# A gated-recurrence layer: the branch product in two halves with two gates behind each, and two PSUM tiles for the gates

## The chip, the cores and the metric

The kernel runs on one core of one Trainium2 chip. The metric is the device time of one execution in microseconds (us); of several executions the median counts. The engines are named as the profile names them: PE is TensorE (matrix products), DVE is VectorE, ACT is ScalarE, POOL is GpSimd, SP is SyncE, which here only issues DMA transfers.

## What is computed

Two layers of a hybrid backbone over 512 latent and 256 context tokens with 1024 channels. The first layer is a bidirectional RG-LRU, the second a retention layer, which the change doesn't touch. Of the reference this is the part that matters:

```python
def rglru_scan(xs, w_r, b_r, w_i, b_i, lam, h0, reverse):
    r = sigmoid(block_product(xs, w_r) + b_r)
    i = sigmoid(block_product(xs, w_i) + b_i)
    log_a = -LRU_C * r * softplus(-lam)
    a = exp(log_a)
    b = sqrt(-expm1(2.0 * log_a)) * (i * xs)
    ...  # h[t] = a[t] * h[t-1] + b[t]

def mixer_lru(h, hc, ...):
    u = h @ w_in                          # 1024 -> 4096: 2048 for x, 2048 for the branch
    xl = dwconv(u[..., :W], conv_w, conv_b, LRU_PAD)
    ...                                   # both directions, context first, then latent
    y = ((lat[0] + lat[1]) * silu(u[..., W:])) @ w_out
```

Each product is made of float32 operands split into a high and a low part, as three matmuls that add up in PSUM.

## The kernel before

Channels lie on the partitions and the 768 tokens (256 context, 512 latent) side by side in a row. The 2048 channels of the recurrence are 16 channel tiles of 128. PSUM is cut into four tiles of 1024 columns (`slots`, L51), which the compiled program names ps_67 to ps_70. The list `rot` with `psum()` (L54) hands them out in rotation.

`iteration(c)` (L447) runs once for each channel tile c = 0 to 15, and works on several tiles at once:

- **x product** of tile c+2: eight blocks of 128 input channels, two halves of 384 tokens, three matmuls each, so 48 matmuls (`mm_in`, L290). `x_post` (L267) is the convolution: one ACT pass (L271) and six DVE passes (L275) that all read the PSUM tile.
- **branch product** of tile c+1 (`w_in[c+1, 1]`), again 48 matmuls. `g_post` (L285) is its SiLU: a sigmoid on ACT (L287) and a product on DVE (L288), which both read the PSUM tile.
- **four gates** of tile c, six matmuls each from the convolved x and its low part (xh, xlo, made by `x_split`, L278). One sigmoid on ACT (L482) reads each.
- **output units** (`wout_unit`, L431): iterations 4, 6, 8, 10, 12, 13, 14 and 15 have one, 5 and 9 have two, 0 to 3, 7 and 11 none (the table `UNITS`, L105). A unit is 48 matmuls on two PSUM tiles, read by four DVE passes (`gate_add`, L242).
- **the recurrence of tile c** on ACT and DVE: exp, tanh and square (L499, L500, L502), square root (L515), products (L503, L504, L518), scans (L520 to L524), the sum with the branch (L530, L531), and the split of the result into yh (ACT, L532) and yl (DVE, L533). Three changes of ACT's function table (ACT_TABLE_LOAD) lie in each iteration.

The order of an iteration on PE is x product, branch product, four gates, units. Each of the first six pieces takes the next PSUM tile of the rotation. With four tiles and no unit, the third gate takes the tile of the x product and the fourth that of the branch product, made just before. From iteration 3 on four tiles rotate; in iterations 1 and 2 the fourth is taken by the modulation's matmuls.

Weights are loaded by SP into a pool of four raw tiles (`wraw`), split into whi (ACT, L91) and wlo (DVE, L96, or ACT L93 and a transfer that adds) in pools of four; `take()` (L154) splits three ahead. In iterations 3 to 14 `row_steps` (L404) also loads rows of the next layer's modulation weights through the same four raw tiles and reduces each in one DVE pass (L414), three an iteration: `mod_pull()` stands behind the x product, behind the branch product and behind the gates.

The sequence on each engine is set by a scheduler from the program's order; each engine runs its own list strictly in order. After iteration 15 the last products of the layer run on the four PSUM tiles in the order `T` (L543); they need yl of tile 15.

Of the kernel before, what the change touches and what calls it, by code (L numbers as in the profile page):

```python
# [15 lines left out]
KD = D // P  # L16
# [3 lines left out]
CT = 16  # L20
# [23 lines left out]
def backbone(ctx: ExitStack, tc: tile.TileContext, xT, vec, trig, lru_mod_sc, lru_mod_gt, lru_w_in, lru_w_g, lru_w_out,  # L44
# [6 lines left out]
    slots = [psp.tile([P, 1024], F32, name=f"ps{i}") for i in range(4)]  # L51
    rot = [0, 1, 2, 3]

    def psum():  # L54
        i = rot.pop(0)
        rot.append(i)
        return slots[i]
# [43 lines left out]
    PULL = {1: 2, 2: 2}  # L101
# [3 lines left out]
    UNITS = {4: [0], 5: [1, 2], 6: [3], 8: [4], 9: [5, 6], 10: [7], 12: [8], 13: [9], 14: [10], 15: [11]}  # L105
# [48 lines left out]
    def take(n=1, ahead=3):  # L154
        i = pos[0]
        pos[0] += n
        split_to(i + ahead)
        got = ready[i:i + n]
        ready[i:i + n] = [None] * n
        return got if n > 1 else got[0]  # L160
# [84 lines left out]
    with ExitStack() as l0:  # L245
# [18 lines left out]
        hs, us, ys = [], {}, {}  # L264
# [20 lines left out]
        def g_post(c, u):  # L285
            t = sil[c] = r3.tile([P, NT], F32, tag="sil", name="sil")
            nc.scalar.activation(out=t, in_=u[:, 128:896], func=AF.Sigmoid)  # L287
            nc.vector.tensor_tensor(out=t, in0=u[:, 128:896], in1=t, op=ALU.mult)  # L288

        def mm_in(w, ps, ks=range(KD)):  # L290
            for k in ks:
                wk = [t[:, k * P:(k + 1) * P] for t in w]
                for a, b in halves:
                    mm3(ps[:, 128 + a:128 + b], wk, cut(hs[k], a, b), k == 0, k == KD - 1)
# [132 lines left out]
        def pull(it, n):  # L427
            for _ in range(n):
                next(it, None)

        def wout_unit(i):  # L431
            g, dp = divmod(i, 4)
            hi, lo = take()
            yk = [ys[4 * g + k] for k in range(4)]
            pss = [psum(), psum()]
            for ks in ((0, 1, 2), (3,)):
                for d in range(2):
                    for k in ks:
                        w = [t[:, k * 256 + d * P:k * 256 + (d + 1) * P] for t in (hi, lo)]
                        for a, b in halves:  # L440
                            mm3(pss[d][:, 128 + a:128 + b], w, cut(yk[k], a, b), k == 0, k == 3)
            for d in range(2):
                dt = 2 * dp + d
                gate_add(acc_c, dt, pss[d][:, 128:384], gate0[0][:, dt, :])
                gate_add(acc_l, dt, pss[d][:, 384:896], gate0[1][:, dt, :])

        def iteration(c):  # L447
            def mod_pull():
                pull(mod_it, PULL.get(c, 0))
                pull(row_it, 1 if c in ROWS else 0)  # L450

            if c == 1:
                rot[:] = [i for i in rot if i != 3]
            if c + 2 < CT:
                us[c + 2] = psum()
                mm_in(take(), us[c + 2])
                if c == 0:
                    g_post(0, gps)
                    x_post(0)
                    x_split(0)  # L460
                    x_post(1)
                x_post(c + 2)
                mod_pull()
            if c + 1 < CT:
                ps = psum()
                mm_in(take(), ps)
                g_post(c + 1, ps)
                mod_pull()
            xh, xlo = xs.pop(c)
            wg = take()  # L470
            ri = []
            units = list(UNITS.get(c, []))
            for q in range(4):
                if q == 2 and c in EARLY:
                    wout_unit(units.pop(0))
                ps = psum()
                w = [t[:, q * P:(q + 1) * P] for t in wg]
                for a, b in halves:
                    mm3(ps[:, 128 + a:128 + b], w, (xh[:, a:b], xlo[:, a:b]), True, True)
                t = e(f"g{q}")  # L480
                boff = (V_BR if q % 2 == 0 else V_BI) + (q // 2) * CT + c
                nc.scalar.activation(out=t, in_=ps[:, 128:896], func=AF.Sigmoid, bias=vt[:, boff:boff + 1])  # L482
                ri.append(t)
            if c + 1 < CT:
                x_split(c + 1)
            mod_pull()
            if c == max(PULL):
                pull(mod_it, 100)
                rot.append(3)
            if c == max(ROWS):  # L490
                pull(row_it, 100)
            for i in units:
                wout_unit(i)
            x = xl.pop(c)
            aa, qq, ix, qs = [], [], {}, {}
            for d in range(2):
                r = ri[2 * d]
                a = e("a")
                nc.scalar.activation(out=a, in_=r, func=AF.Exp, scale=sneg[:, d * CT + c:d * CT + c + 1])  # L499
                nc.scalar.activation(out=r, in_=r, func=AF.Tanh, scale=spos[:, d * CT + c:d * CT + c + 1])  # L500
                q = e("q")
                nc.scalar.activation(out=q, in_=a, func=AF.Square)  # L502
                ix[d] = nc.vector.tensor_tensor(out=ri[2 * d + 1], in0=ri[2 * d + 1], in1=x, op=ALU.mult)  # L503
                qs[d] = nc.vector.scalar_tensor_tensor(out=q, in0=q, scalar=1.0, in1=r, op0=ALU.add, op1=ALU.mult)  # L504
                aa.append(a)
                qq.append(q)
            if c == CT - 1:
                with tc.issue_after(ix[1].ins):
                    split_to(pos[0] + 3, dve=True)
                yt = [(yp.tile([P, NT], F32R, tag="yh", name="yh"), yp.tile([P, NT], F32R, tag="yl", name="yl")) for _ in range(3)]  # L510
                with tc.issue_after(qs[0].ins):
                    split_y(pos[0] + 4, yt, 0, True)
            for d in range(2):
                i, q, a = ri[2 * d + 1], qq[d], aa[d]
                nc.scalar.activation(out=q, in_=q, func=AF.Sqrt)  # L515
                if d and c < CT - 1:
                    nc.scalar.activation(out=warm, in_=q[:, 0:1], func=AF.Sigmoid)
                nc.vector.tensor_tensor(out=i, in0=i, in1=q, op=ALU.mult)  # L518
                if d == 0:
                    nc.vector.tensor_tensor_scan(out=q, data0=a, data1=i, initial=0.0, op0=ALU.mult, op1=ALU.add)  # L520
                else:
                    nc.vector.tensor_tensor_scan(out=q[:, 0:NC][:, ::-1], data0=a[:, 0:NC][:, ::-1],
                                                 data1=i[:, 0:NC][:, ::-1], initial=0.0, op0=ALU.mult, op1=ALU.add)
                    nc.vector.tensor_tensor_scan(out=q[:, NC:NT][:, ::-1], data0=a[:, NC:NT][:, ::-1],  # L524
                                                 data1=i[:, NC:NT][:, ::-1], initial=q[:, 0:1], op0=ALU.mult, op1=ALU.add)
            s, sl = qq[0], sil.pop(c)
            yh = yp.tile([P, NT], F32R, tag="yh", name="yh")
            yl = yp.tile([P, NT], F32R, tag="yl", name="yl")
            for a, b in ([(NC, NT), (0, NC)] if c == CT - 1 else [(0, NT)]):
                nc.vector.tensor_tensor(out=s[:, a:b], in0=s[:, a:b], in1=qq[1][:, a:b], op=ALU.add)  # L530
                nc.vector.tensor_tensor(out=s[:, a:b], in0=s[:, a:b], in1=sl[:, a:b], op=ALU.mult)  # L531
                nc.scalar.activation(out=yh[:, a:b], in_=s[:, a:b], func=AF.Copy)  # L532
                nc.vector.tensor_tensor(out=yl[:, a:b], in0=s[:, a:b], in1=yh[:, a:b].bitcast(F32), op=ALU.subtract)  # L533
            ys[c] = (yh, yl)
            if c == CT - 1:
                split_y(pos[0] + 5, yt, 1, False)
# [3 lines left out]

        base = pos[0]
        l0x.close()
        T = [slots[i] for i in (2, 3, 1, 0)]  # L543

        def half(t, d):
            return T[t][:, 512 * d:512 * d + 512]

# [37 lines left out]
        def ctx_mm(dt):  # L585
            return last_mm(T[dt // 4][:, 256 * (dt % 4):256 * (dt % 4) + 256], dt, range(4), slice(0, NC))

# [17 lines left out]
        def ctx_add(q):  # L605
            for j in range(4):
                dt = 4 * q + j
                gate_add(acc_c, dt, T[q][:, 256 * j:256 * j + 256], gate0[0][:, dt, :])

# [329 lines left out]
def _pack(i):  # L939
    import numpy as np  # L940

    def cols(a, n):
        return np.asarray(a).reshape(n, P).T

# [25 lines left out]
def _layout(i):  # L970
# [11 lines left out]
    rwo = g['ret_w_out'].reshape(4, 4, P, 4, 256).transpose(0, 3, 2, 1, 4).reshape(4, 4, P, 1024)  # L982
    xT = np.concatenate([g['ctx'][0], g['x'][0]], axis=0).T
    mw = g['lru_mod_w']
# [24 lines left out]
```

## Time and profile before

| | us |
|---|---|
| median of three runs | 1080.85 |
| the three runs | 1078.47, 1080.85, 1082.74 |
| the profiled execution | 1081.35 |
| its span, first to last instruction | 1079.5 |
| PE busy | 1049.4 |
| DVE busy | 709.7 |
| ACT busy | 604.1 |

The profiled execution lies 0.50 us above the median, and 1.85 us of it lie outside the span. PE's busy time counts each matmul to its modelled end, so what it could still gain is read from the gaps before its instructions and from the length of like stretches. The stretches used below run from the first gate of iteration c to the first gate of iteration c+1: they hold the gates and units of c, the x product of tile c+3 and the branch product of tile c+2.

### The profile page before, as it was taken

The numbers are of one execution on the slowest core, as the hardware profiler recorded it, in microseconds if no ns is written. First come the engines' busy times: TensorE is split into PE (matmuls) and PEld (weight loads), VectorE is DVE, ScalarE is ACT, GpSimd is POOL, SyncE is SP. The second block draws the span as 40 slices with busy tenths as digits, with TensorE's granted clock in tenths as the row PEclk, the third lists the DMA queues.
The fourth block names the chain that finished last, engine by engine and source line by source line (L and its number), as shares of the span: only waits on it lengthen the run. The fifth ranks groups of instructions, "written<-read, shape, count | busy, mean of one in ns | idle before, by whom it ended". The sixth has DMA issues, their size and how long they took to land.

```text
span 1079.5 us, 14058 instructions
## 1 busy us (share of the span) xinstructions
PE 1049.4 (97%) x5644; PEld 934.1 (87%) x5644; DVE 709.7 (66%) x1031; ACT 604.1 (56%) x782; POOL 29.1 (3%) x37
## 2 busy tenths in 40 slices
PE   8999999999999999999999999999999999999997
PEld 7898898899999999998888788888888888887887
DVE  4777668876687787888889836444554535643366
ACT  5557888777788578888364534124432234322354
POOL 0000000000000000000000000000000000000000
PEclk9999999999999999999999999999999999999999
DMA  9623637665757666432113412212122021220202
GB/s 359 231 81 113 190 78 209 178 166 148 187 161 173 162 165 156 122 109 78 50 56 124 154 67 71 94 40 78 39 78 98 20 79 59 75 97 4 78 1 78
DMA packets 36243, 121.71 MB, mean 113 GB/s; under 512 B 3793, under 2 KB 6993, under 8 KB 35153
## 3 DMA queue, kind: packets, MB, share of 16 engines
q1 hardware_dynamic: 31568, 104.03, 27.8%
q0 software_dynamic: 4608, 16.78, 9.1%
q8 instruction: 44, 0.72, 0.3%
q14 instruction: 23, 0.18, 0.1%
HBM read 118.70 MB, written 2.10 MB: 112 GB/s over the span
## 4 chain that ended last, share of the span: by engine, by line
PE 68%; DVE 13%; ACT 12%; issue 4%; DMA 3%; SPq 0%; DVEq 0%; ACTq 0%
PE ps L76 23%; PE ps L77 22%; PE ps L78 21%; DVE xl L275 2%; ACT a L499 2%; ACT g L500 2%; DVE g L518 2%; ACT g L482 2%; ACT q L502 1%; ACT L499 1%; ACT L515 1%; DVE q L524 1%; DMA wraw<-in_ret_mod_w_dram 1%; ACT q L515 1%; DVE q L530 1%
## 5 line engine op out<-in xcount | busy, mean ns | idle before, releaser
L76 PE MATMUL ps<-hl,whi 128*128 128x384 f32 (+2 forms) x816 | 284.9, 350 | 3.0 <-ACT g L482 1.5
L78 PE MATMUL ps<-hh,wlo 128*128 128x384 f32 (+2 forms) x816 | 282.8, 347 | 0.1
L77 PE MATMUL ps<-hh,whi 128*128 128x384 f32 (+2 forms) x816 | 282.9, 347 | 0.0
L91 ACT ACTIVATE whi<-wraw 128x1024 fp32r<-128x1024 f32 (+1 forms) x125 | 125.1, 1002 | 189.9 <-PE ps L77 163.5
L76 PEld LDWEIGHTS ps<-hl,whi 128*128 128x128 f32 x816 | 153.4, 188 | 19.1 <-DVE hl L239 3.1
L78 PEld LDWEIGHTS ps<-hh,wlo 128*128 128x128 f32 x816 | 153.4, 188 | 10.3 <-DVE wlo L96 0.6
L77 PEld LDWEIGHTS ps<-hh,whi 128*128 128x128 f32 x816 | 153.5, 188 | 9.5
L76 PE MATMUL ps<-yl,whi 128*128 128x384 f32 (+2 forms) x416 | 143.8, 348 | 3.9 <-DVE yl L533 1.8
L96 DVE TENSOR_TENSOR wlo<-wraw,whi 128x1024 fp32r<-128x1024 f32 (+1 forms) x94 | 106.1, 1130 | 59.6 <-ACT whi L91 58.2
L77 PE MATMUL ps<-yh,whi 128*128 128x384 f32 (+2 forms) x416 | 143.3, 345 | 0.0
L78 PE MATMUL ps<-yh,wlo 128*128 128x384 f32 (+2 forms) x416 | 141.6, 343 | 0.0
L76 PEld LDWEIGHTS ps<-yl,whi 128*128 128x128 f32 x416 | 78.6, 189 | 12.7 <-ACT g L482 3.0
L78 PEld LDWEIGHTS ps<-yh,wlo 128*128 128x128 f32 x416 | 78.8, 190 | 5.7
L77 PEld LDWEIGHTS ps<-yh,whi 128*128 128x128 f32 x416 | 78.9, 190 | 5.2
L76 PE MATMUL ps<-wlo,hh 128*128 128x512 f32 x192 | 75.1, 394 | 1.4 <-DVE rb L705 0.9
L77 PE MATMUL ps<-whi,hh 128*128 128x512 f32 x192 | 74.9, 390 | 0.0
L78 PE MATMUL ps<-whi,hl 128*128 128x512 f32 x192 | 74.3, 389 | 0.0
L482 ACT ACTIVATE g<-ps,vt 128x768 f32<-128x768 f32 x64 | 55.3, 898 | 5.4 <-PE ps L78 3.6
L275 DVE SCALAR_TENSOR_TENSOR xl<-ps,vt,xl 128x255 f32<-128x255 f32 (+1 forms) x96 | 54.3, 602 | 2.2 <-ACT xl L271 2.2
L76 PE MATMUL ps<-xlo,whi 128*128 128x384 f32 x128 | 45.0, 354 | 10.2 <-DVE xl L275 5.8
L414 DVE SCALAR_TENSOR_TENSOR wraw<-wraw,cr 128x1024 f32<-128x1024 f32 x32 | 39.0, 1218 | 17.4 <-DMA wraw<-in_ret_mod_w_dram 12.5
L504 DVE SCALAR_TENSOR_TENSOR q<-q,g 128x768 f32<-128x768 f32 x32 | 30.5, 954 | 28.5 <-ACT q L502 28.5
(208 smaller groups left out, 1647.9 us busy)
## 6 DMA issues: line engine op xcount, KB each, us to landing
wraw<-in_ret_w_in_dram SPq DMA_DIRECT2D x48, 512.0 KB, 3.5
wraw<-in_lru_w_in_dram SPq DMA_DIRECT2D x32, 512.0 KB, 4.5
wraw<-in_ret_mod_w_dram SPq DMA_DIRECT2D x32, 512.0 KB, 4.2
wlo<-in_lru_w_in_dram POOLq DMA_DIRECT2D x22, 512.0 KB, 5.7
mraw<-in_lru_mod_sc_dram SPq DMA_DIRECT2D x8, 1024.0 KB, 8.9
wraw<-in_lru_w_out_dram SPq DMA_DIRECT2D x16, 512.0 KB, 3.6
wraw<-in_ret_w_out_dram SPq DMA_DIRECT2D x16, 512.0 KB, 4.0
wlo<-in_lru_w_out_dram POOLq DMA_DIRECT2D x10, 512.0 KB, 5.6
```

Of the source, the lines that this page charges most:

```text
L76: nc.tensor.matmul(ps, lhsT=lhs[0], rhs=rhs[1], start=first, stop=False)
L77: nc.tensor.matmul(ps, lhsT=lhs[0], rhs=rhs[0], start=False, stop=False)
L78: return nc.tensor.matmul(ps, lhsT=lhs[1], rhs=rhs[0], start=False, stop=last)
L91: nc.scalar.activation(out=hi, in_=raw, func=AF.Copy)
L96: last_split[0] = nc.vector.tensor_tensor(out=lo, in0=raw, in1=hi.bitcast(F32), op=ALU.subtract)
L275: nc.vector.scalar_tensor_tensor(out=t[:, o0:o1], in0=u[:, o0 + sh:o1 + sh], scalar=cw[j], in1=t[:, o0:o1], op0=ALU.mult, op1=ALU.add)
L414: nc.vector.scalar_tensor_tensor(out=raw, in0=raw, scalar=1.0, in1=cr, op0=ALU.mult, op1=ALU.mult, accum_out=m1[:, f, t:t + 1])
L482: nc.scalar.activation(out=t, in_=ps[:, 128:896], func=AF.Sigmoid, bias=vt[:, boff:boff + 1])
L499: nc.scalar.activation(out=a, in_=r, func=AF.Exp, scale=sneg[:, d * CT + c:d * CT + c + 1])
L500: nc.scalar.activation(out=r, in_=r, func=AF.Tanh, scale=spos[:, d * CT + c:d * CT + c + 1])
L504: qs[d] = nc.vector.scalar_tensor_tensor(out=q, in0=q, scalar=1.0, in1=r, op0=ALU.add, op1=ALU.mult)
L515: nc.scalar.activation(out=q, in_=q, func=AF.Sqrt)
```

## The change

From iteration 3 on the branch product is made in two halves of four input blocks (24 matmuls each). Gates 0 and 1 stand between the halves and gates 2 and 3 behind the second, and `g_post` with its `mod_pull()` moves behind the second half. Gates 0 and 2 share one PSUM tile, gates 1 and 3 a second (`gs`), which are neither the x product's nor the branch product's, wherever four tiles are free. With three free tiles (iterations 1 and 2) the gates alternate between the one that is left and the x product's. `rot` is rewritten by hand for the units, for the next iteration and for the products after the loop (`tail`).

```diff
+            xs_, ys_ = (rot.pop(0) if c + 2 < CT else None), (rot.pop(0) if c + 1 < CT else None)
+            units = list(UNITS.get(c, []))
+            if c == 0:
+                gs = [1, 2, 3, 0]
+                rot[:] = [1, 2, 0]
+            elif len(rot) == 1:
+                gs = [rot[0], xs_] * 2
+                rot[:] = gs[:2] + [ys_]
+            else:
+                gs = [rot.pop(0), rot.pop(0)] * 2
+                rest = sorted((i for i in range(4) if i not in gs), key=lambda i: i == ys_)
+                rot[:] = gs[:2] + rest if c >= CT - 2 else [rest[0]] + gs[:2] + [rest[1]]
+            mid = KD // 2 if c > max(PULL) else KD
...
-            if c + 1 < CT:
-                ps = psum()
-                mm_in(take(), ps)
-                g_post(c + 1, ps)
-                mod_pull()
+            if ys_ is not None:
+                wy = take()
+                mm_in(wy, slots[ys_], range(mid))
+                if mid == KD:
+                    g_post(c + 1, slots[ys_])
+                    mod_pull()
...
             for q in range(4):
+                if q == 2 and ys_ is not None and mid < KD:
+                    mm_in(wy, slots[ys_], range(mid, KD))
+                    g_post(c + 1, slots[ys_])
+                    mod_pull()
                 if q == 2 and c in EARLY:
+                    rot[:] = rest + gs[:2]
                     wout_unit(units.pop(0))
+                    tail[:] = [rest[0], gs[0], gs[1], rest[1]]
+                wg = wg or take()
-                ps = psum()
+                ps = slots[gs[q]]
...
-                rot.append(3)
+                rot.insert(0, 3)
...
-        T = [slots[i] for i in (2, 3, 1, 0)]
+        T = [slots[i] for i in tail]
```

What this does to the engines' lists is seen in three places. Names read output<-inputs; g is a gate, sil the branch's sigmoid, and the lines of the changed kernel are higher by 22 to 26.

ACT, iteration 3, before, from the weight splits to the table load of the recurrence:

```order
L93 ACTIVATE wlo<-whi 128x1024
L91 ACTIVATE whi<-wraw 128x512
L482 ACTIVATE g_1488<-ps_67,vt 128x768
L482 ACTIVATE g_1496<-ps_70,vt 128x768
L281 ACTIVATE xh<-xl 128x768
L532 ACTIVATE yh<-q 128x768
L287 ACTIVATE sil<-ps_69 128x768
L482 ACTIVATE g_1504<-ps_68,vt 128x768
L91 ACTIVATE whi<-wraw 128x1024
L482 ACTIVATE g_1512<-ps_69,vt 128x768
L499 ACT_TABLE_LOAD
```

The same place of the changed kernel:

```order
L91 ACTIVATE whi<-wraw 128x1024
L504 ACTIVATE g_1458<-ps_67,vt 128x768
L93 ACTIVATE wlo<-whi 128x1024
L91 ACTIVATE whi<-wraw 128x512
L504 ACTIVATE g_1466<-ps_68,vt 128x768
L504 ACTIVATE g_1504<-ps_67,vt 128x768
L558 ACTIVATE yh<-q 128x768
L287 ACTIVATE sil<-ps_69 128x768
L504 ACTIVATE g_1512<-ps_68,vt 128x768
L525 ACT_TABLE_LOAD
```

Four gates on four tiles, the last of them the branch's own ps_69, became four gates on ps_67 and ps_68, with three of them ahead of yh and sil.

ACT, iteration 14 (the last branch product, one unit), before:

```order
L517 ACTIVATE warm<-q 128x1
L91 ACTIVATE whi<-wraw 128x1024
L532 ACTIVATE yh<-q 128x768
L287 ACTIVATE sil<-ps_67 128x768
L482 ACTIVATE g_4215<-ps_70,vt 128x768
L482 ACTIVATE g_4223<-ps_68,vt 128x768
L482 ACTIVATE g_4231<-ps_69,vt 128x768
L91 ACTIVATE whi<-wraw 128x1024
L482 ACTIVATE g_4239<-ps_67,vt 128x768
L499 ACT_TABLE_LOAD
```

And of the changed kernel:

```order
L543 ACTIVATE warm<-q 128x1
L504 ACTIVATE g_4184<-ps_70,vt 128x768
L504 ACTIVATE g_4192<-ps_67,vt 128x768
L558 ACTIVATE yh<-q 128x768
L91 ACTIVATE whi<-wraw 128x1024
L287 ACTIVATE sil<-ps_68 128x768
L504 ACTIVATE g_4231<-ps_70,vt 128x768
L504 ACTIVATE g_4239<-ps_67,vt 128x768
L91 ACTIVATE whi<-wraw 128x1024
L525 ACT_TABLE_LOAD
```

Gates 0 and 1 moved ahead of yh; gates 2 and 3 still stand behind yh, a weight split and sil.

SP's queue of transfers around iteration 7, before (in_ret_mod_w are the rows of the next layer's modulation):

```order
L82 DMA wraw<-in_ret_mod_w_dram 128x1024
L82 DMA wraw<-in_lru_w_in_dram 128x1024
L82 DMA wraw<-in_ret_mod_w_dram 128x1024
L82 DMA wraw<-in_lru_w_in_dram 128x1024
L82 DMA wraw<-in_ret_mod_w_dram 128x1024
L82 DMA wraw<-in_lru_w_g_dram 128x512
```

And of the changed kernel:

```order
L82 DMA wraw<-in_ret_mod_w_dram 128x1024
L82 DMA wraw<-in_lru_w_in_dram 128x1024 x2
L82 DMA wraw<-in_ret_mod_w_dram 128x1024 x2
L82 DMA wraw<-in_lru_w_g_dram 128x512
```

The rows no longer alternate with the weights; two of an iteration's three stand back to back, ahead of the gates' weights.

## Rows read from the trace of the kernel before

**Rows 1.** PE on the page: busy us, share of the span, instructions.
```profile
PE 1049.4 (97%) x5644; PEld 934.1 (87%) x5644; DVE 709.7 (66%) x1031; ACT 604.1 (56%) x782; POOL 29.1 (3%) x37
```
**Rows 2.** PE's waits over the span: total us, times, longest us.
```profile
PE ps L76 <- DVE xl L275: 5.8, 6, 2.6
PE ps L76 <- DVE sil L288: 4.0, 4, 1.4
PE ps L76 <- ACT g L482: 3.4, 5, 1.4
```
**Rows 3.** Stretches: length, busy us of PE, PEld, DVE, ACT, POOL; clock, DMA, GB/s.
```profile
129.68:152.82 23.14, 22.30 (x130) 21.89 (x129) 11.93 (x14) 20.02 (x24) 0.86 (x1) 1.00 0.44 120
152.82:175.93 23.11, 21.44 (x122) 20.77 (x122) 21.29 (x33) 19.10 (x24) 1.76 (x2) 1.00 0.59 163
175.93:211.28 35.35, 31.33 (x170) 30.72 (x169) 29.80 (x40) 27.93 (x33) 3.49 (x4) 0.95 0.63 177
211.28:251.21 39.93, 38.26 (x217) 37.65 (x217) 30.23 (x43) 26.48 (x30) 3.48 (x4) 1.00 0.68 168
251.21:280.53 29.32, 29.32 (x169) 29.32 (x169) 22.91 (x31) 23.40 (x27) 2.60 (x3) 1.00 0.64 170
280.53:302.10 21.57, 21.17 (x122) 20.85 (x121) 12.39 (x16) 20.47 (x24) 0.86 (x1) 1.00 0.50 130
302.10:332.74 30.64, 29.79 (x170) 29.21 (x169) 26.75 (x38) 24.75 (x30) 3.50 (x4) 1.00 0.71 184
332.74:371.77 39.03, 38.04 (x217) 37.72 (x217) 29.58 (x42) 26.04 (x30) 3.49 (x4) 1.00 0.66 168
452.93:474.35 21.42, 21.27 (x121) 20.95 (x121) 19.05 (x26) 17.68 (x21) 0.00 (x0) 1.00 0.37 103
```
**Rows 4.** PE timeline, gates of iterations 4, 5 and 8: start, us, [idle before].
```profile
180.83 0.66 PE L76 MATMUL ps<-xlo,whi 128*128 128x384 f32 x1 [2.63 <-DVE xl L275]
190.83 0.45 PE L76 MATMUL ps<-xlo,whi 128*128 128x384 f32 x1 [1.39 <-DVE sil L288]
216.51 0.44 PE L76 MATMUL ps<-xlo,whi 128*128 128x384 f32 x1 [1.23 <-DVE sil L288]
307.54 0.44 PE L76 MATMUL ps<-xlo,whi 128*128 128x384 f32 x1 [0.85 <-DVE xl L275]
```
**Rows 5.** The stretch behind the longest of these waits, columns as in rows 3.
```profile
180.83:184.10 3.27, 3.27 (x10) 3.27 (x11) 3.24 (x5) 3.27 (x5) 1.25 (x2) 0.50 0.67 101
```
**Rows 6.** Groups of the page: busy, mean ns, idle before and its releaser.
```profile
L91 ACT ACTIVATE whi<-wraw 128x1024 fp32r<-128x1024 f32 (+1 forms) x125 | 125.1, 1002 | 189.9 <-PE ps L77 163.5
L482 ACT ACTIVATE g<-ps,vt 128x768 f32<-128x768 f32 x64 | 55.3, 898 | 5.4 <-PE ps L78 3.6
```
**Rows 7.** ACT timeline behind the gates of iteration 7.
```profile
286.42 0.88 ACT L482 ACTIVATE g<-ps,vt 128x768 f32<-128x768 f32 x1
287.32 1.28 ACT L499 ACT_TABLE_LOAD   x1
```
**Rows 8.** DVE timeline: end of that recurrence and of the convolution beside it.
```profile
305.88 0.94 DVE L531 TENSOR_TENSOR q<-q,sil 128x768 f32<-128x768 f32 x1
306.75 0.74 DVE L275 SCALAR_TENSOR_TENSOR xl<-ps,vt,xl 128x511 f32<-128x511 f32 x1
```
**Rows 9.** ACT timeline, table loads of iterations 13 and 14; PE's last wait.
```profile
459.47 1.28 ACT L499 ACT_TABLE_LOAD   x1
...
483.05 1.28 ACT L499 ACT_TABLE_LOAD   x1
...
521.26 0.51 PE L76 MATMUL ps<-yl,whi 128*128 128x512 f32 x1 [1.76 <-DVE yl L533]
```
**Rows 10.** Modulation rows: DVE's waits for them, the issue list, the chain.
```profile
DVE wraw L414 <- DMA wraw<-in_ret_mod_w_dram: 12.5, 11, 2.5
...
wraw<-in_ret_mod_w_dram SPq DMA_DIRECT2D x32, 512.0 KB, 4.2
...
180.96 6.74 DMA wraw<-in_ret_mod_w_dram
```

More of the change, by code (lines that the diff above doesn't have):

```diff
@@ L445, in wout_unit @@
                 gate_add(acc_l, dt, pss[d][:, 384:896], gate0[1][:, dt, :])
+        tail = []
         def iteration(c):
@@ L453, in iteration @@
                 rot[:] = [i for i in rot if i != 3]
-            if c + 2 < CT:
-                us[c + 2] = psum()
+            xs_, ys_ = (rot.pop(0) if c + 2 < CT else None), (rot.pop(0) if c + 1 < CT else None)
[11 more added lines that the diff above has]
+            mid = KD // 2 if c > max(PULL) else KD
+            if xs_ is not None:
+                us[c + 2] = slots[xs_]
                 mm_in(take(), us[c + 2])
@@ L463, in iteration @@
                 mod_pull()
-            if c + 1 < CT:
-                ps = psum()
-                mm_in(take(), ps)
-                g_post(c + 1, ps)
-                mod_pull()
+            if ys_ is not None:
[4 more added lines that the diff above has]
+                    mod_pull()
             xh, xlo = xs.pop(c)
-            wg = take()
+            wg = None
             ri = []
-            units = list(UNITS.get(c, []))
             for q in range(4):
+                if q == 2 and ys_ is not None and mid < KD:
+                    mm_in(wy, slots[ys_], range(mid, KD))
+                    g_post(c + 1, slots[ys_])
+                    mod_pull()
                 if q == 2 and c in EARLY:
+                    rot[:] = rest + gs[:2]
                     wout_unit(units.pop(0))
-                ps = psum()
+                    tail[:] = [rest[0], gs[0], gs[1], rest[1]]
+                wg = wg or take()
+                ps = slots[gs[q]]
                 w = [t[:, q * P:(q + 1) * P] for t in wg]
@@ L488, in iteration @@
                 pull(mod_it, 100)
-                rot.append(3)
+                rot.insert(0, 3)
             if c == max(ROWS):
                 pull(row_it, 100)
+            if c == CT - 2:
+                rot[:] = rest + gs[:2]
             for i in units:
                 wout_unit(i)
+            if c == CT - 2:
+                rot[:] = gs[:2] + rest
             x = xl.pop(c)
```

## The prediction

> **What bounds the kernel now.** I read the page first: PE is busy 97% of the span [rows 1], so only what PE waits for can be won. The list of its waits puts the convolution's DVE passes (L275), the branch's SiLU (L288) and the gates' sigmoids on top [rows 2]; all three are readers of a PSUM tile that PE wants to fill again. That list counts from modelled matmul ends, so I sized the waits another way, from the stretches between first gates [rows 3]. Iteration 6 is the clean one: 29.32 us for 168 matmuls of 384 columns, PE busy throughout, so 0.1745 us a matmul. From it follow the lengths without any wait: 120 x 0.1745 = 20.94 us where there is no unit, 37.70 us where there are two. What each stretch is above that is what PE lost there: iteration 3 23.11 - 20.94 = 2.2, iteration 4 35.35 - 29.32 = 6.0, iteration 5 39.93 - 37.70 = 2.2, iteration 7 0.6, iteration 8 1.3, iteration 9 1.3, iteration 13 0.5 [rows 3]. Iteration 10 is like 6 (nothing), 11 like 7 (I take 0.2), 12 like 8. Iteration 2 is 2.2 above [rows 3], of which I put 0.8 down to the modulation's own matmuls there. In all about 17 us, 1.6% of the time: the ceiling. The timeline then says which tile was missing: gate 2 waits for L275 on the x product's tile, gate 3 for L288 on the branch's [rows 4]. Those are the two tiles that the change takes from the gates.
>
> **The change part by part.** No work is added or removed: the matmuls, ACT and DVE passes and transfers are the same in number and size. What moves:
>
> Gates 2 and 3, tiles. Gate 2 now needs gate 0's sigmoid, not the convolution. Between gate 0's last matmul and gate 2 stand gate 1 and half a branch product, 30 x 0.1745 = 5.2 us; a sigmoid takes 0.90 us [rows 6]. So the wait is gone if ACT reaches that sigmoid in time. ACT's order after the change has the sigmoids of gates 0 and 1 ahead of sil everywhere. In an iteration without a unit ACT is nearly as full as PE (20.47 of 21.57 us [rows 3]), so I checked that case with iteration 7: its table load starts 2.0 us after the last gate's matmuls (one weight split and one sigmoid [rows 6, 7]), the sigmoid of the next gate 0 would end some 17 us after them, and PE wants the tile 18.8 us after them (x product, half a branch product, two gates, the other half: 108 x 0.1745). Covered, by under 2 us. The moved gate product also needs its xlo earlier by half a product, 4.2 us; it is made in the middle of the recurrence and is early enough.
>
> Iterations 5, 7, 9, 11 and 13 lose what they lose to the tiles of x and branch alone, so all of it goes: 2.2 + 0.6 + 1.3 + 0.2 + 0.5 = 4.8 us.
>
> Iterations 1 and 2 have three tiles; gate 1 still waits for the convolution, gate 2 no longer for sil. I take 1.0 us (between 0.3, the small waits, and 1.4, all).
>
> Iteration 3. In ACT's new order the split of the gates' weights (L91, 512 wide) stands between the sigmoids of gates 0 and 1. It needs a buffer that the branch product's second half still reads, so gate 1's sigmoid ends about 0.2 + 0.6 + 0.9 = 1.7 us after that half, and gate 3 wants its tile 1.05 us after it: a wait of 0.7, with lateness on ACT some 1.4. Saved 0.8 of 2.2 (0 to 2.2).
>
> Iterations 4, 8 and 12 follow one without a unit, and here is what comes late next. The first half of the unit takes the x product's tile, and the convolution must have read it. In iteration 8 that reading ends at 306.75 + 0.74 = 307.49 [rows 8], 20.2 us after the table load at 287.32 [rows 7], so 22.2 us after the last gate's matmuls; the ACT and DVE chain that leads there is the same after the change. PE reaches the unit 20.94 us after those matmuls. So 1.3 us of wait replace the 1.3 us that iterations 8 and 12 lose now: nothing won. In iteration 4 the chain also holds more passes over modulation rows; I take a wait of 2.0 us in place of 6.0. A wait of 2.63 us was followed by ten matmuls at a granted clock of 0.50 [rows 5], the level of 1.2 GHz, after full clock before: 3.27 us where ten take 1.75, so 1.5 us. That is in the 6.0; a wait of 2.0 may or may not bring it back, so I take 3.6 us saved (2.5 to 5.0).
>
> Iterations 14, 15 and the products behind them. Here the chain of ACT and DVE sets the end, not PE. Now the table loads of iterations 13 and 14 start 23.58 us apart [rows 9]. After the change gates 2 and 3 of iteration 14 stand behind yh of tile 13, a weight split and sil in ACT's list. yh waits for L531, which ends 19.5 us after the table load with a convolution beside it (305.88 + 0.94 - 287.32 [rows 7, 8]) and some 18.8 without; with six more ACT passes (yh, a split, sil, two sigmoids, a split) at 0.88 us each, a sigmoid's length [rows 7], the next table load comes 24.1 us after the one before: 0.5 later than now. From there to the last yl the chain is the same, and PE, early, waits longer than its 1.76 us [rows 9]. So what iterations 14 and 15 lose isn't won, and 0.5 is paid.
>
> Sum: 4.8 + 1.0 + 0.8 + 3.6 + 0 - 0.5 = 9.7 us off the profiled execution's own 1081.35: 1071.65. That execution lies 0.50 above the median of the runs, so I expect a median of 1071.15, and say 1071.
>
> **A rule against it.** PE's waits in the rows are for tiles whose readers are six DVE passes or a sigmoid and a product [rows 2, 4], while a gate's single reader takes 0.90 us [rows 6]. The Trainium skill (Trace Analysis, Optimizing Tensor Performance, Matmuls) says that independent groups should rotate through different PSUM banks, so that reading one out overlaps the next group's matmuls. By it the change, from four tiles to two for the gates, goes the wrong way; the trace so far bears out another reading, that rotating into tiles with slow readers is what costs. What it would give stands as the third rival.
>
> **The rivals.** *All waits go.* If the recurrence starts earlier because two sigmoids are done earlier, the units of 4, 8 and 12 don't wait either: 17 us, 1064. Against it: the table load follows the last gate's sigmoid, which doesn't come earlier.
>
> *The chain sets the pace everywhere.* Only the waits for sil (4.0 us [rows 2]) are won, since ACT at 20.47 of 21.57 us and DVE at 29.80 of 35.35 [rows 3] have no room: 1077. For it: the two are fullest where PE waits most. Against it: iterations 5 and 9, with DVE at 30 of 39 us, lose over 1 us each all the same.
>
> *Two tiles are too few.* Gate 2 waits for a sigmoid as gate 2 waits now: two sigmoids less a gate, 1.8 - 1.05 = 0.75 us, in 13 iterations 9.8 us, which eats the gain: 1081. Against it: the 5.2 us of cover.
>
> *The modulation rows hold DVE up (slower).* Two rows now stand back to back in SP's queue, ahead of the gates' weights. DVE has waited 12.5 us for rows in 11 places, the longest 2.5, a row lands 4.2 us after its issue, and the chain once shows 6.74 [rows 10]. If DVE stands still for 6.0 us more in each iteration, x_post is later by that in iterations 4, 8 and 12 (18 us on PE), and L531, on which yh waits ahead of the gates' sigmoids in ACT's list, eats the room behind a unit: 18.8 + 48 x 0.1745 = 27.2 us until PE wants the tile, less 21.5 for L531 and 1.8 for two ACT passes, 3.9 (five iterations, 2.1 us each, 10.5 us). That is 1071 + 28.5 = 1099; at 4.2 us a time, 1085. It decides for slower than before from 3.3 us a time. Against it: the passes over the rows stand in the same places of DVE's list as before.
>
> **How the numbers follow.** My forecast 0.64, all waits go 0.08, chain everywhere 0.16, two tiles too few 0.03, rows hold DVE up 0.09. The forecast's own bounds: 2.5 to 5.0 in iteration 4, 0.3 to 1.4 in 1 and 2, 0 to 2.2 in 3, 3.5 to 4.8 in the five, -2 to 0.5 at the end: 4 to 14 us saved, 1067 to 1077. The range 1065 to 1080 takes in the chain (1077) and leaves out 1064 and the slower case. What a measurement of this kernel can tell from no change is about 0.5%, 5.4 us, so faster means under 1075.4: 0.64 + 0.08 = 0.72; same 0.16 + 0.03 = 0.19; slower 0.09.
>
> **What would show it.** In the profile after: no waits of gates for L275 or L288 from iteration 3 on; stretches without a unit at 21 us, with two at 37.7; a wait of a unit's first matmul (yl) for L275 of 1.3 us in iterations 8 and 12 and about 2 in 4; a longer wait for yl at the end, near 3 us. I am wrong if gates 2 and 3 wait for sigmoids, if iterations 5 and 9 keep their loss, or if DVE's waits for modulation rows grow well over 12.5 us.

## The result, and the profile after

The changed kernel takes 1073.68 us (median; 1070.61 to 1076.48), the kernel before 1078.92 us beside it: a ratio of 0.9941, 95% interval 0.9917 to 0.9965. Two later measurements on other occasions gave 1072.78 us (0.9932, interval 0.9913 to 0.9951) and 1071.46 us (0.9928, interval 0.9909 to 0.9948). So 5 to 9 us are won where the prediction had 9.7. The profiled span is 1072.9 us, 6.6 less than before.

The page's row for PE after the change, which answers to [rows 1]:

```profile
PE 1044.6 (97%) x5644; PEld 931.6 (87%) x5644; DVE 709.7 (66%) x1031; ACT 603.4 (56%) x782; POOL 29.1 (3%) x37
```

The share reads the same as before, since the span and PE's busy time fell together, by 6.6 and 4.8 us. The list of PE's waits tells more (after the change, columns as in [rows 2]; L504 is the gate's sigmoid, L275 a convolution pass, L559 yl; L288, sil, is gone from it):

```profile
PE ps L76 <- DVE xl L275: 5.7, 5, 1.9
PE ps L209 <- DVE ssum L320: 2.7, 1, 2.7
PE ps L76 <- ACT g L504: 2.2, 4, 0.9
...
PE ps L76 <- DVE yl L559: 1.7, 2, 1.3
```

L275 still costs 5.7 us, but at another place: who waits now is mostly a unit (three of the five waits, 4.8 us), and no longer a gate of an iteration from 3 on. The stretches between the first gates of iterations say which (after the change, columns as in [rows 3]: length, busy us of PE, PEld, DVE, ACT, POOL, clock, DMA share, GB/s; iterations 3, 4, 5, 7, 8, 9, 11, 12 and 13):

```profile
149.15:172.06 22.91, 21.40 (x122) 20.76 (x121) 21.52 (x29) 22.26 (x29) 1.76 (x2) 1.00 0.57 150
172.06:203.55 31.49, 29.60 (x170) 29.27 (x170) 30.51 (x43) 28.69 (x34) 3.13 (x4) 1.00 0.79 211
203.55:241.32 37.77, 37.77 (x218) 37.77 (x217) 28.45 (x40) 26.14 (x30) 3.03 (x5) 1.00 0.67 167
...
270.65:292.69 22.04, 21.15 (x122) 20.83 (x122) 15.89 (x23) 16.34 (x20) 0.89 (x2) 1.00 0.59 154
292.69:323.75 31.06, 29.59 (x170) 29.27 (x170) 29.59 (x40) 29.13 (x35) 3.09 (x4) 1.00 0.67 168
323.75:361.52 37.77, 37.77 (x218) 37.77 (x217) 28.15 (x40) 26.16 (x30) 3.09 (x5) 1.00 0.66 165
390.85:412.27 21.42, 21.15 (x122) 20.83 (x122) 16.67 (x24) 16.34 (x20) 0.88 (x2) 1.00 0.64 165
412.27:443.34 31.07, 29.60 (x170) 29.27 (x169) 28.92 (x38) 27.26 (x32) 2.62 (x3) 1.00 0.63 153
443.34:464.35 21.01, 21.01 (x122) 21.01 (x122) 18.24 (x27) 17.02 (x21) 0.00 (x0) 1.00 0.32 101
```

Against the lengths without a wait (20.94, 29.32, 37.70 us), iterations 5, 9 and 13 are clean. Iterations 7 and 11 are longer than before (22.04 for 21.57, 21.42 for 21.16), and so are 8 and 12 (31.06 for 30.64). Here is iteration 8's wait: PE's timeline where the last gate ends and the unit begins (start, us, what, in brackets the idle time before and its releaser):

```profile
300.91 0.34 PE L78 MATMUL ps<-xh,wlo 128*128 128x384 f32 x1
302.71 0.44 PE L76 MATMUL ps<-yl,whi 128*128 128x384 f32 x1 [1.47 <-DVE xl L275]
```

The bracket counts from a modelled end. The waits that the text gives without a bracket go from start to start, less the 0.17 us that a matmul takes: 302.71 - 300.91 - 0.17, so 1.63 us here.

And here is what is new in iteration 7. VectorE's timeline from the end of iteration 6's recurrence, then SyncE's issues:

```profile
267.31 0.67 DVE L548 TENSOR_TENSOR_SCAN q<-a,g 128x256 f32<-128x256 f32 x1
271.07 1.23 DVE L414 SCALAR_TENSOR_TENSOR wraw<-wraw,cr 128x1024 f32<-128x1024 f32 x1 [3.09 <-DMA wraw<-in_ret_mod_w_dram]
272.22 0.08 DVE L414 DVE_READ_ACCUMULATOR wraw<-wraw,cr 128x1 f32 x1
272.22 1.28 DVE L550 TENSOR_TENSOR_SCAN q<-a,q,g 128x512 f32<-128x512 f32 x1
...
275.31 0.95 DVE L557 TENSOR_TENSOR q<-q,sil 128x768 f32<-128x768 f32 x1
```

```profile
264.01 0.33 SPq L82 DMA_DIRECT2D wraw<-in_ret_mod_w_dram  x1
```

ScalarE and PE behind it:

```profile
276.29 0.85 ACT L558 ACTIVATE yh<-q 128x768 fp32r<-128x768 f32 x1 [6.89 <-DVE q L557]
277.04 1.67 ACT L504 ACTIVATE g<-ps,vt 128x768 f32<-128x768 f32 x2
```

```profile
277.98 0.45 PE L76 MATMUL ps<-xlo,whi 128*128 128x384 f32 x1 [0.89 <-ACT g L504]
```

Read from the bottom: gate 2 waits for gate 0's sigmoid; the sigmoid stands behind yh on ScalarE, which had been idle for 6.89 us; yh waits for L557; L557 stands behind the last scan; and in front of that scan stands a pass over a modulation row for which VectorE stood still for 3.09 us. The row was issued at 264.01, just as the pass over the row before it ended, and landed 7.0 us later. Before the change the pass stood behind that recurrence, ahead of the convolution.

### The profile page after: what moved, and what is told of

The parts are those of the page before. It is cut to its first block, busy times and chain, and to the rows that moved or that the text cites. A ratio compares the mean times of both kernels' runs of the same rounds, so it can differ in the third digit from the quotient of the medians.

```text
span 1072.9 us, 14016 instructions
## 1 busy us (share of the span) xinstructions
PE 1044.6 (97%) x5644; PEld 931.6 (87%) x5644; DVE 709.7 (66%) x1031; ACT 603.4 (56%) x782; POOL 29.1 (3%) x37
## 4 chain that ended last, share of the span: by engine, by line
PE 72%; DVE 12%; ACT 9%; DMA 4%; issue 2%; SPq 0%; DVEq 0%
PE ps L76 24%; PE ps L77 23%; PE ps L78 23%; DMA wraw<-in_ret_mod_w_dram 3%; ACT g L504 2%; DVE xl L275 1%; DVE q L550 1%; DVE wraw L414 1%; ACT a L525 1%; DVE g L544 1%; ACT g L526 1%; ACT q L528 1%; ACT whi L91 1%; DMA acc_l<-in_xT_dram 1%; DVE q L557 1%
## 5 line engine op out<-in xcount | busy, mean ns | idle before, releaser
L504 ACT ACTIVATE g<-ps,vt 128x768 f32<-128x768 f32 x64 | 55.6, 895 | 8.9 <-PE ps L78 8.9
L275 DVE SCALAR_TENSOR_TENSOR xl<-ps,vt,xl 128x255 f32<-128x255 f32 (+1 forms) x96 | 54.6, 604 | 1.7 <-ACT xl L271 1.7
L688 DVE TENSOR_TENSOR vl<-ps,vh 128x512 fp32r<-128x512 f32 x24 | 16.4, 689 | 49.2 <-ACT vh L687 49.2
L414 DVE SCALAR_TENSOR_TENSOR wraw<-wraw,cr 128x1024 f32<-128x1024 f32 x32 | 39.0, 1221 | 13.3 <-DMA wraw<-in_ret_mod_w_dram 11.7
L76 PEld LDWEIGHTS ps<-wlo,hh 128*128 128x128 f32 x192 | 36.0, 188 | 12.2 <-DVE rb L731 2.6
```

The costliest lines, as they stand in the source:

```text
L76: nc.tensor.matmul(ps, lhsT=lhs[0], rhs=rhs[1], start=first, stop=False)
L275: nc.vector.scalar_tensor_tensor(out=t[:, o0:o1], in0=u[:, o0 + sh:o1 + sh], scalar=cw[j], in1=t[:, o0:o1], op0=ALU.mult, op1=ALU.add)
L414: nc.vector.scalar_tensor_tensor(out=raw, in0=raw, scalar=1.0, in1=cr, op0=ALU.mult, op1=ALU.mult, accum_out=m1[:, f, t:t + 1])
L688: nc.vector.tensor_tensor(out=lo, in0=src, in1=hi.bitcast(F32), op=ALU.subtract)
```

## The experiments

**Which part gains.** Two runs do one part alone. Own tiles for the gates, the branch product whole:

```diff
-            mid = KD // 2 if c > max(PULL) else KD
+            mid = KD
```

> The gates have two tiles of their own, but the branch product is made whole ahead of all four gates. Theory 'order and tiles are needed together': gate 2 wants gate 0's tile 1.05 us after gate 0, and the sigmoid of 0.90 us stands behind sil and often a weight split on ScalarE, so gates 2 and 3 wait for sigmoids, 0.5 to 1 us in each of 13 iterations: 1080 to 1087 us, and the list of PE's waits shows some ten waits for the sigmoid (L504). Theory 'the tiles alone carry the gain': 1074 us as the changed kernel, iterations 5 and 9 at 37.8 us, no more waits for sigmoids than its four.

1075.52 us, ratio 0.9957 (0.9941 to 0.9972): the tiles alone carry more than half of the changed kernel's gain, and my theory that the two belong together fell. This kernel also keeps the modulation rows where they were, which the change does not (see the pair of rows, below). From the first gate of iteration 4 to that of 13 it saves 6.3 us (277.00 to 270.68), where the whole change saves 5.7, 6.7 and 6.3 in its three traces. Iterations 4, 5 and 9 of that kernel (stretches as above), and its waits for sigmoids:

```profile
174.46:206.88 32.42, 29.86 (x169) 29.20 (x169) 31.44 (x44) 25.86 (x31) 3.49 (x4) 1.00 0.79 200
206.88:244.81 37.93, 37.93 (x218) 37.72 (x218) 26.52 (x38) 25.60 (x29) 3.49 (x4) 1.00 0.65 161
326.00:363.93 37.93, 37.93 (x218) 37.72 (x218) 27.61 (x40) 25.60 (x29) 3.49 (x4) 1.00 0.68 164
```

```profile
PE ps L76 <- ACT g L504: 4.6, 6, 1.3
```

A sigmoid of 0.90 us fits beside a gate of 1.05 us, so two tiles that are read in 0.90 us cost 0.2 us an iteration where ScalarE is on time. In iterations 3, 4 and 14 a gate waits 1.1 to 1.3 us for a sigmoid.

The other part alone: the kernel before with its rotation through four tiles, and the product in two halves.

```diff
-                mm_in(take(), ps)
-                g_post(c + 1, ps)
-                mod_pull()
+                mid = KD // 2 if c > max(PULL) else KD
+                wy, py = take(), ps
+                mm_in(wy, py, range(mid))
...
+                if q == 2 and c + 1 < CT and mid < KD:
+                    mm_in(wy, py, range(mid, KD))
+                    g_post(c + 1, py)
+                    mod_pull()
```

> The branch product is made in two halves with two gates behind each, but the gates still rotate through all four tiles. Theory 'order and tiles are needed together': gate 3 takes the branch product's tile 1.05 us after its second half, while sigmoid and product of the SiLU take about 1.9 us with nothing ahead of them and more with yh and a split ahead: 1 to 2 us lost in each iteration from 3 to 14, against about 4 us won on the convolution's tile: 1085 to 1097 us, waits for sil (L288's line) the largest. Theory 'the order alone carries the gain': 1074 us.

1079.8 us, ratio 0.9997 (0.9985 to 1.0009): nothing, as neither theory had it. The gates did wait for sil (3.8 us in 5 waits), but the scheduler that sets PE's order put matmuls of the unit or of the next product between gates 2 and 3, which filled most of the wait I had priced. The largest single wait was a new one, in iteration 4. Here it is, with that iteration's stretch and VectorE's waits for modulation rows:

```profile
181.72 0.42 PE L76 MATMUL ps<-xlo,whi 128*128 128x384 f32 x1 [4.53 <-ACT whi L91]
```

```profile
170.74:207.88 37.14, 31.38 (x169) 30.76 (x169) 30.57 (x40) 31.05 (x37) 2.61 (x3) 0.95 0.71 182
```

```profile
DVE wraw L414 <- DMA wraw<-in_ret_mod_w_dram: 21.4, 16, 3.4
```

So this run doesn't show what the split is worth by itself. Its edit also moves `mod_pull()` behind the second half, and VectorE's waits for rows grew from 12.5 to 21.4 us. One of 3.38 us ends at 172.07, in front of a recurrence's product and the convolution, some 10 us ahead of that gate; that it makes the gate wait is likely but not shown. Iteration 4 takes 37.14 us where 35.35 stood before; 5 to 12 together take 2.0 us less than before. The split with the rows apart and the old rotation was not run.

**Why units wait for the convolution.** Between the last three convolution passes of iteration 8, VectorE does L556 and L557, which finish the recurrence of iteration 7 (VectorE's timeline of the changed kernel):

```profile
299.15 0.72 DVE L275 SCALAR_TENSOR_TENSOR xl<-ps,vt,xl 128x511 f32<-128x511 f32 x1
299.79 0.94 DVE L556 TENSOR_TENSOR q<-q 128x768 f32<-128x768 f32 x1
300.65 0.47 DVE L275 SCALAR_TENSOR_TENSOR xl<-ps,vt,xl 128x255 f32<-128x255 f32 x1
301.05 0.95 DVE L557 TENSOR_TENSOR q<-q,sil 128x768 f32<-128x768 f32 x1
301.91 0.74 DVE L275 SCALAR_TENSOR_TENSOR xl<-ps,vt,xl 128x511 f32<-128x511 f32 x1
```

The edit puts them behind these passes, in iterations 4, 8 and 12 (finish holds L556 to L559 and is called behind gates 0 and 1 of the next iteration):

```diff
+                if q == 2 and pend:
+                    finish(*pend.pop())
...
+            if c in (3, 7, 11):
+                pend.append((c, qq))
+            else:
+                finish(c, qq)
```

> The changed kernel with one thing moved: in iterations 4, 8 and 12 the sum of the two scans and its product with sil (L556, L557 of the changed kernel, 0.95 us each), of the iteration before, stand on VectorE behind the last convolution pass in place of between the last three. Theory 'the unit waits for VectorE's order': the last pass ends 1.9 us earlier, the unit's waits of 2.06, 1.63 and 1.63 us fall to about 0.2, 0 and 0: 5 us less than the changed kernel, 1069 us. Rival 'the lateness only moves': yh, behind the sum on ScalarE, holds sil and the two sigmoids up by the same 1.9 us, the next table load is later, and iterations 5, 9 and 13 or 12's follower lose what was won: 1073 to 1074 us.

1069.18 us, ratio 0.9893 (0.9874 to 0.9911). That is 3.6 us less than the changed kernel beside it (1072.78). By the traces of these two, iterations 4, 8 and 12 are 4.9 us shorter and iteration 7 is 1.1 us shorter; against that, a second fall of TensorE's clock stands in this run's trace and not in the other's (last section). The unit's first matmul now follows the last gate with no gap (PE's timeline in iteration 8), and iterations 4, 7, 8 and 12 are 29.45, 21.09, 29.33 and 29.33 us long:

```profile
298.58 0.34 PE L78 MATMUL ps<-xh,wlo 128*128 128x384 f32 x1
298.75 0.35 PE L76 MATMUL ps<-yl,whi 128*128 128x384 f32 x1
```

```profile
172.72:202.17 29.45, 29.45 (x169) 29.27 (x169) 28.71 (x41) 26.59 (x32) 2.61 (x3) 1.00 0.77 201
269.27:290.36 21.09, 21.09 (x121) 20.83 (x121) 15.35 (x23) 16.33 (x20) 0.90 (x2) 1.00 0.65 158
290.36:319.69 29.33, 29.33 (x169) 29.26 (x169) 27.83 (x38) 28.32 (x35) 2.63 (x3) 1.00 0.65 165
407.67:437.00 29.33, 29.33 (x169) 29.33 (x169) 27.56 (x37) 26.79 (x32) 2.63 (x3) 1.00 0.66 161
```

The lateness didn't move elsewhere: iterations 5 and 9 take 37.78 us, as before the edit (37.77). The wait of iteration 7 had gone to 0.1 us as well, though nothing was moved there: the row came earlier in that kernel, and VectorE stood still for 2.27 us in front of it, not 3.09. So that wait hung on the row.

**The pair of rows.** The change also put the second modulation row of an iteration right ahead of the third in SyncE's queue, since its pull went with the branch product's second half. The edit pulls it where it was, ahead of the gates:

```diff
                 if mid == KD:
                     g_post(c + 1, slots[ys_])
-                    mod_pull()
+                mod_pull()
...
                     g_post(c + 1, slots[ys_])
-                    mod_pull()
```

> The changed kernel with the second modulation row of each iteration pulled where it stood before the change: ahead of the gates and the branch product's second half, so that rows are not two in a row in SyncE's queue. Theory 'the pair of rows is what came late in iteration 7': gate 2's wait there (1.05 and 1.23 us in two profiles) goes to below 0.2, the rest is unchanged: 1072 us, and VectorE's longest wait for a row falls from 3.1 us to about 2.5. Rival 'the pass stands ahead of the scan wherever the row is pulled': the wait stays at 1 us, 1073 us.

1069.13 us, ratio 0.9906 (0.9882 to 0.9929): 2 to 5 us less than the changed kernel's three medians, and 2.9 to 3.9 by the stretches of iterations 4, 7, 8, 11 and 12 against its three traces, about three times what I expected. Iterations 4, 7, 8 and 12, and VectorE's waits for rows:

```profile
170.87:200.92 30.05, 29.58 (x169) 29.25 (x169) 28.56 (x39) 27.97 (x33) 3.13 (x4) 1.00 0.76 203
268.02:288.90 20.88, 20.88 (x121) 20.88 (x121) 12.11 (x18) 16.89 (x20) 1.74 (x2) 1.00 0.70 191
288.90:319.58 30.68, 29.60 (x169) 29.28 (x169) 29.10 (x40) 28.87 (x35) 3.09 (x4) 1.00 0.65 166
407.56:438.23 30.67, 29.60 (x170) 29.27 (x170) 28.72 (x38) 26.99 (x32) 2.62 (x3) 1.00 0.60 155
```

```profile
DVE wraw L414 <- DMA wraw<-in_ret_mod_w_dram: 6.0, 6, 1.5
```

Gate 2 of iteration 7 doesn't wait any more, and in VectorE's order the pass stands behind the product with sil again. Iteration 4 gained 1.4 us (0.8 and 1.6 against the two other traces) and iterations 8 and 12 0.4 us each, which I had not expected: the chain that ends in the convolution was late by the pair as well. What is left in 8 and 12 is 1.35 us over 29.32, near the prediction's 1.3.

Is it the rows' work or their place? Two runs of one kernel leave the rows out: their transfers, their passes, and so the shift and gain that they make, which are set to constants.

> Leaves out the modulation rows of the retention part (the transfers of ret_mod_w and cr, the 32 passes of 1.22 us over them, the sigmoids of cr, and so the shift and gain that they make, which are set to constants); all else as in the changed kernel. Theory 'a late row holds iteration 7': there VectorE waited 3.1 us for a row whose transfer took 7.0 us, in front of the last scan, and yh, behind the scan on ScalarE, held gate 0's sigmoid: gate 2's wait of 1.05 us in iteration 7 goes to 0, and so does what is left in 11. Theory 'iterations 8 and 12 are short on VectorE's order, not on rows': their waits for L275 stay at 1.6 us, while those of 3 and 4 shrink by 1 us each. Sum: 3 to 4 us less than the changed kernel, 1069 to 1070 us. Rival 'the rows are what is late everywhere': 8 and 12 go to 0 too, 1066 us.

> Leaves out the modulation rows once more (transfers, passes and the sigmoids of cr), for a profile that wasn't disturbed. Theory 'rows cost by their place, not by their work': gate 2 of iteration 7 waits under 0.2 us, the units of 8 and 12 still wait for L275, 1.2 to 1.6 us, as with the rows apart: 1069 to 1070 us. Rival 'the work counts too': the units' waits fall below 0.5 us and the time to 1066 us.

1070.57 us (ratio 0.9908, 0.9884 to 0.9931) in the first; the trace read here is that of the second, whose execution took 1070.01 us. No wait in iterations 7 and 11 (20.88 us each), while iterations 8 and 12 take 30.68 and 30.67 us, as with the rows apart. So 39 us of passes and 16.8 MB of transfers cost PE nothing that this kernel shows, as long as they aren't in front of the wrong scan; and the units' 1.35 us are VectorE's order, which recur_late takes away.

**More of the same.** The sum of the scans behind the convolution in all iterations from 4 to 13, and the same with the first step of the rows behind the gates in iteration 3:

> As the run with the sum of the scans behind the convolution, in all iterations from 4 to 13 in place of 4, 8 and 12; yh then stands behind the sigmoids of gates 0 and 1 on ScalarE everywhere. Theory 'gate 2 of iteration 7 waits since yh stands ahead of the sigmoid': its wait is gone whenever the row comes, and no gate waits from iteration 4 to 14: 1068 to 1069 us, as the run with three iterations or up to 1 us less. Rival 'yh late holds sil and the sigmoids of gates 2 and 3': iterations 5, 6, 9, 10 and 13 begin to lose over 0.3 us each: 1070 to 1072 us.

> As the run before, and in iteration 3 the first step of the modulation rows (two sigmoids of 0.6 us over cr) is pulled behind the gates, with two rows after it. Theory 'those two sigmoids stand ahead of gate 0's sigmoid and make iteration 3 late': gate 3's wait of 1.0 us there goes, and of the 0.8 us of the next product for L275 a part: 1.0 to 1.8 us less, 1067 us. Rival 'it comes back in iteration 4, whose chain then holds the rows': 1068 to 1070 us, with a wait for L275 of about 1 us in iteration 4.

1069.19 us (0.9901, 0.9878 to 0.9925) and 1070.87 us (0.9907, 0.9886 to 0.9929). The first is no better than three iterations: all gates are on time, but the units of 4, 8 and 12 wait 0.65 to 0.76 us again. In the second, gate 3's wait of iteration 3 does go, as its theory says, but the next product's grows from 0.8 to 1.4 us, and 22.92 us become only 22.58; the rival was right on where it goes: iteration 4, in whose chain it put the rows' passes, waits 1.0 and 2.0 us and takes 34.08 us in place of 30.19, of which some 1.6 us is a fall of the clock.

**Both moves that gained, and the changed kernel again.**

> The changed kernel with both moves that gained: the second modulation row pulled ahead of the gates, and in iterations 4, 8 and 12 the sum of the scans behind the convolution. Theory 'two separate losses': the row's pairing cost iteration 7 its 1.05 us, 11 up to 0.4 and the units about 0.4 to 0.8 each, VectorE's order the rest of the units' waits, so the sum is all of them: no wait for L275 over 0.3 us from iteration 4 to 14 and stretches of 29.3 us there, 1066 to 1067 us. Rival 'one loss counted twice': each move alone already takes what there is, 1069 us as either.

1066.41 us (1065.21 to 1068.91), ratio 0.9883 (0.9865 to 0.9901), the lowest median of all. Iterations 4, 7, 8 and 12:

```profile
170.07:199.63 29.56, 29.56 (x170) 29.27 (x170) 28.79 (x40) 28.96 (x34) 2.62 (x3) 1.00 0.77 212
266.73:287.61 20.88, 20.88 (x122) 20.88 (x122) 12.11 (x18) 16.89 (x20) 1.74 (x2) 1.00 0.70 191
287.61:316.93 29.32, 29.32 (x169) 29.32 (x169) 27.79 (x38) 28.45 (x35) 2.63 (x3) 1.00 0.65 163
404.91:434.24 29.33, 29.33 (x170) 29.33 (x169) 26.53 (x36) 26.43 (x32) 2.63 (x3) 1.00 0.56 147
```

That the two moves take two separate losses isn't shown by this. From the first gate of iteration 4 to that of 13, both_moves takes 264.17 us (170.07 to 434.24) and recur_late 264.28 (172.72 to 437.00), and PE is busy throughout in both: moving the sums had already taken what the rows cost there. The ratios, 0.9883 and 0.9893, can't be told apart either. What the profiled executions differ by lies elsewhere: besides the falls at start and end that both have, recur_late's trace has two, in iteration 3 and at 561 us. In recur_late's six runs the time goes roughly with the granted clock, from 1070.51 us at 0.993 to 1064.92 us at 0.998; both_moves had 1065.21 us at 0.997.

> The changed kernel once more, for its second profile: 1070 to 1077 us. If the wait for the first statistics (L209 for ssum, 2.7 us against 1.7 before) belongs to the single execution and not to the change, it differs again here, by up to 1 us either way; the waits of iterations 3, 4, 7, 8, 11 and 12 return within 0.2 us.

> The changed kernel a third time, beside the run before: 1071 to 1076 us. TensorE's clock fell in iteration 3 in one of its two profiles (1.6 us lost) and not in the other: if that hangs on the single execution, it may be either here, after the same two waits of 1.0 and 0.8 us.

The times are above. In the two further traces iteration 7 is 22.22 and 21.75 us long, iterations 8 and 12 31.0 to 31.1, iteration 4 30.87 and 31.61: these waits belong to the kernel. Iteration 11 is 20.90 and 21.00: its wait doesn't. Nor does the wait for the first statistics, 2.2 and 1.8 us there. The clock's fall is told below.

## Why the prediction was right or wrong

Forecast and measurement by place, as us saved in the stretches of the profiled execution (before less after; where the new order moves 24 matmuls over a border, their 4.19 us are taken off):

| place | forecast | measured |
|---|---|---|
| 5, 9, 13 | 2.2 + 1.3 + 0.5 | 2.2 + 1.3 + 0.4 |
| 7, 11 | 0.6 + 0.2 | -0.5 - 0.3 |
| 1 and 2 | 1.0 | 0.7 |
| 3 | 0.8 | 0.2 |
| 4 | 3.6 | 3.9 |
| 8, 12 | 0 | -0.4 - 0.4 |
| 14, 15 and the products up to the last yl | -0.5 | 0.5 |
| sum | 9.7 | 7.6 |

The span gained 6.6: the first gate of iteration 1 came 1.2 us later, 1.0 us of it by a longer wait for ssum that the change doesn't touch, and behind the last yl 0.2 us came back. That the sum comes within some 2 us of the forecast is in part luck: 7 and 11 fell 1.6 us short of it, 8 and 12 0.8 and iteration 3 0.6, while the end gave 1.0 more.

*Right:* the tiles are what the gates lost by, and iterations 5, 9 and 13 gained what they had lost. In iteration 4 the unit's wait came where it was put and with its size, 2.06 us (1.43 and 2.18 in the other traces).

*The step that failed* is a sentence under the rivals: that the passes over the rows stand in the same places of VectorE's list as before. In iteration 7 one stood ahead of the last scan of iteration 6 in place of behind L531. I had put L531's end at 21.5 us behind the last gate's matmuls, 19.5 of it behind the table load, and found 3.9 us of room for gate 2. In the trace these matmuls end at 249.72, the table load starts at 252.45, and L557, the same product, ends 23.8 us behind the load: 4.3 us later than I had it, with 0.7 more ahead of the load, and the wait is 1.05. With the rows apart the kernel takes 1069.13 us, 10 to 11 us less than before: a little more than the forecast of 9.7. So the sum was about right for a kernel without the pair of rows, and the rows' rival was right in its mechanism with its price far too high: 2.9 to 3.9 us in all, not 14 to 28.

*A telltale that was blind:* I would have called the rows harmless as long as VectorE's waits for them didn't grow well over 12.5 us. They were 11.7 us in 9 places after the change, less than before, and 6.0 with the rows apart. What made iteration 7 wait was one of them, of 3.09 us, in front of a scan that others wait for.

*Iteration 3:* gate 3's wait for its sigmoid was forecast at 0.7 to 1.4 us and is 1.01. Not foreseen was the next wait, 0.82 us: there is no unit in iteration 3, so the next x product is what takes the tile that the convolution still reads.

*Iterations 8 and 12:* 1.3 us of wait were forecast, 1.63 measured, and 1.24 with the rows apart: the term was short by what the pair of rows added, 0.4 us.

*The tail:* the table loads of iterations 13 and 14 start at 453.63 and 476.69, 23.06 us apart where 24.1 were forecast and 23.58 stood before. L557 came 18.0 us behind the table load, not 18.8, and the passes up to the next one took 5.1 us, not 5.3. The wait for the last yl fell to 1.3 us; it was to grow to 3.

*Two tiles too few* had 0.75 us lost in each of 13 iterations. The changed kernel's gates wait 2.2 us for sigmoids in four places, and even in tiles_alone, where nothing covers the sigmoids, it is 0.2 us in 5 and 9 and over 1 us only in iterations 3, 4 and 14. The Trainium skill (Perfetto Trace Analysis, Optimizing Tensor Performance, Matmuls) says that independent groups of matmuls should rotate through different PSUM banks, so that reading one out overlaps the next group's matmuls. Here the number of tiles didn't decide, but who reads them: two tiles that are read in one pass of 0.90 us (tiles_alone, 1075.52 us) do better than four of which one is read by VectorE's six passes and one by a sigmoid and a product (1080.08 us beside it).

What stays open: what the product's split is worth by itself. tiles_alone has the rows apart and takes 1075.52 us, row_apart has the split besides and takes 1069.13, but some of these 6 us is the clock's: the trace of tiles_alone has two falls behind the loop, at 513 and 568 us. From the first gate of iteration 4 to that of 13, where the clock falls in neither trace, row_apart is 3.3 us shorter (270.68 to 267.36), and 2.4 us of that is iteration 4, which differs by 0.7 us between traces of one kernel.

## What to carry to other kernels

Give a short group of matmuls a PSUM tile that is read by one fast pass, and keep it off tiles that a chain of passes reads; two are enough where the pass is shorter than the group. When work is moved, look up on every engine in order what now stands ahead of a step that others wait for: two transfers put one behind the other, with a pass over a late one ahead of a scan, took away about a third of this gain, while the sum of waits for such transfers fell. And of what an engine does between two passes that release a tile, ask whether anyone waits for it: two VectorE operations put behind the convolution were worth at least half as much as the whole change.

## What the runs showed of the hardware

TensorE's granted clock falls after short waits in some executions and not in others of the same kernel. In iteration 3 the changed kernel has the same two waits of 1.0 and 0.8 us, 1.2 us apart, in all three traces; behind them, in the first and in the second trace (windows, columns as in [rows 3]):

```profile
158.00:160.00 2.00, 1.33 (x8) 1.02 (x7) 2.00 (x4) 1.44 (x3) 0.00 (x0) 1.00 0.94 129
160.00:162.00 2.00, 2.00 (x13) 2.00 (x12) 2.00 (x4) 1.98 (x3) 0.00 (x0) 1.00 0.68 133
```

```profile
158.00:160.00 2.00, 1.84 (x7) 1.84 (x8) 2.00 (x4) 1.98 (x4) 0.00 (x0) 0.66 1.01 197
160.00:162.00 2.00, 2.00 (x8) 2.00 (x7) 2.00 (x4) 1.99 (x3) 0.00 (x0) 0.50 0.31 31
```

PE is busy in both, but does 13 matmuls in 2 us at full clock and 8 at 0.50, the level of 1.2 GHz. Such a fall lasted some ten matmuls and cost about 1.5 us where it came in these iterations: behind these waits in changed_again, recur_late and row_apart, not in changed_third, recur_late_all or both_moves; behind the 2.63 us of the kernel before [rows 4, 5], but not behind 2.06 and 2.18 us at the same place after the change. Behind the loop it came after a wait of 2.03 us in recur_late (561 us) and not after one of 2.17 us at the same place of the changed kernel's first trace. So a wait of 1 to 3 us may cost 1.5 us more than itself, and a single trace can't price it. Two executions of one kernel differ by that much.
